# Five shorter steps for the substitution, three for the way back of the inverses, and a step of its own for the transposes

## The chip, the core and the metric

The kernel runs on one core of a Trainium2 chip. The time is the device time of the whole program, in microseconds (us), as a median of several runs. The profile shows one execution: the engines TensorE (PE, with its weight loads as PEld), VectorE (DVE), ScalarE (ACT), GpSimd (POOL) and SyncE (SP, which here issues every DMA). L794 is line 794 of the kernel.

## The reference

One layer of a decoder: the input x (2048 x 1024) is normalised and multiplied by one wide weight matrix. The result feeds three mixers: RWKV-7 time mixing with 8 heads of 64, a short convolution, and causal pooling; each is gated, multiplied by a branch matrix, merged by sigmoid gates, and goes through an output product. The change touches the RWKV part alone. There, in the reference,

```python
def _rwkv7_step(state, inp):
    r_t, w_t, k_t, v_t, a_t, b_t = inp
    sa = jnp.einsum('bhvk,bhk->bhv', state, a_t)
    state = (state * w_t[:, :, None, :] + sa[..., None] * b_t[:, :, None, :]
             + v_t[..., None] * k_t[:, :, None, :])
    y_t = jnp.einsum('bhvk,bhk->bhv', state, r_t)
    return state, y_t
```

runs over all 2048 positions.

## The kernel before, in words

**Main work.** The 2048 columns are worked in two halves. A list, `program` (L1221 to L1266), names the jobs in order: for each half the input projections of the RWKV part, of the convolution (8 pairs), of the pooling (4 pairs) and of the gates (12 pairs), and at the end the products that merge the branches and the output products. Almost every job is a `Pair` (L189): two column blocks of weights times two column blocks of data by Strassen's seven products. One `product` (L179) is 12 matmuls of 128x128 by 128x512: each number is split in a high and a low part, and three of the four products are taken. The weights come by DMA (L149), are split by ScalarE (L141) and GpSimd (L143), and `supply` (L162) keeps them up to five, three and two pieces ahead of their use. The results leave PSUM through ScalarE copies (L233, L238, L243) and VectorE additions (L247, L251, L255); two banks each (`ch` and `mm`) take them in turn.

**Slots.** After each product a job yields, and `execute` (L1280) then calls `supply`, issues the stores that are due (`after_product`), and advances the job's sides. A `Side` (L1076) is a generator with a rate: the rate is added to a credit at each slot, and the generator is called as often as the credit allows, at its first slot once more. At rate 1 that is one call per slot. Each engine executes in the order in which its instructions were issued, so a slot's side work stands ahead of the eviction of the product before it.

**Groups.** The RWKV part is a side: `rwkv_groups` (L674) works 16 groups of 128 positions, 8 in each half, in chunked form. The head (`group_head`, L595) loads and scales, the tail (`group_tail`, L639) normalises the output; the head of the next group and the tail of the one before run along in the group's steps. `step` (L688) yields to the main work, so the number of steps is the number of slots that a group takes: 25 in the first half and 24 in the second. In order of the steps `rwkv_group` (L683) does this:
- The matrices G by matmuls (L711) and a mask (L714), two steps. BK is turned by matmuls (L593), two steps; with them the 32x32 diagonal blocks are stored to DRAM (L734) and loaded back in another layout, NBt (L743). Two steps pass.
- The forward substitution for the inverses of 16x16 triangles (L751 to L757): 15 iterations on VectorE, each a product (L754) and a sum (L755), the operations shrinking from 120 to 8 elements a partition. A step follows j = 3, 7 and 11, and one the end, with which the next head starts.
- The inverses Tt go to DRAM (L763) and come back in the layout TT (L766), a step between. Then `step(3 if g < 8 else 2)` (L767).
- The inverses are put together to 64x64: transposes Td (L771), matmuls bx (L779), a ScalarE copy X (L782), matmuls by (L786), four ScalarE copies into TT (L790), two VectorE transposes T1 (L794), matmuls b1 (L805), copies M1 (L808), matmuls b2 (L812), copies into TT (L815). A step follows Td, X, T1, M1 and the last copies; by, its copies and T1 share one.
- Twice (two chunks of 64): matmuls and a copy R (L829, L832), matmuls and an operation U (L835, L837), matmuls for the new state bS and the output (L843 to L856), with a step after each.

The groups of the second half start with the last job of its RWKV projections and are ended by `groups[1].finish` ahead of the eighth merge job; those of the first half end by the last of the second half's RWKV projections. `finish` issues at once what is left. The loads of the second half's y (`late`, L1258) begin with the seventh merge job.

Of the kernel before, what the change touches and what calls it, by code (L numbers as in the profile page):

```python
# [23 lines left out]

OPS = ("B11", "T1", "T2", "B21", "B22", "T3", "T4")
NB = TH // BLK
# [27 lines left out]
def trunk_kernel(ctx, tc, x, pre_norm_w, post_norm_w, w_in, mu_shift, rwkv_w0, rwkv_w_up,  # L54
# [39 lines left out]
    def mm_bank():  # L94
        return ps.tile([P, BLK], F32, tag="mm", name="mm", bufs=2)
# [7 lines left out]
    def bc(ap, axis, n):  # L103
        u = ap.unsqueeze(axis)
        shape = list(u.shape)
        shape[axis] = n
        return u.to_broadcast(shape)
# [63 lines left out]
    def take():  # L171

        supply(1)
        taken[0] += 1
        return ready.pop(0)
# [3 lines left out]
    def product(bank, wt, op, start, stop=True):  # L179
        (hi, lo), (th, tl) = wt, op[:2]  # L180
        for k in range(HK):
            pe.matmul(bank, hi[:, k, :], th[k], start=start and k == 0, stop=False, skip_group_check=True)  # L182
            pe.matmul(bank, hi[:, k, :], tl[k], start=False, stop=False, skip_group_check=True)  # L183
            pe.matmul(bank, lo[:, k, :], th[k], start=False, stop=stop and k == HK - 1, skip_group_check=True)  # L184
# [4 lines left out]
    class Pair:  # L189
# [37 lines left out]
        def run(self):  # L227
# [6 lines left out]
            bb = mm_bank()  # L234
            product(bb, take(), ops["T1"], True)
            yield
# [52 lines left out]
    def single(ops, c, sink):  # L289

        def body():
# [6 lines left out]
            act.copy(p1[:, 16:], ba)  # L298
            product(bb, a1, h["T1"], True, False)
            yield  # L300
# [91 lines left out]
    def first_ops(x0):  # L392
# [18 lines left out]
        for j in range(4):  # L411
# [10 lines left out]
            def put(o, t, eng):  # L422
                hi, lo = ops[o]
                t3 = t.rearrange("p (k t) -> p k t", k=HK)
                act.copy(hi[:, :, c0], t3)
                ins = eng.tensor_tensor(lo[:, :, c0], t3, hi[:, :, c0].bitcast(F32), ALU.subtract).ins
                if eng is pool:
                    last_lo[0] = ins
# [7 lines left out]
            put("T2", t2, LO[2])  # L436
            put("T1", t1, LO[3])
            put("T3", t3, LO[4])
# [31 lines left out]
    def stage_sums(block, dst):  # L470

        for k in range(2 * HK):
# [8 lines left out]
            yield  # L481
            for o, out_, a, b in (("T1", B[0, 0], B[0, 1], B[0, 0]), ("T3", B[0, 1], B[1, 1], B[0, 1]),
                                  ("T2", B[1, 1], B[1, 1], B[0, 0]), ("T4", B[1, 0], B[1, 0], B[1, 1])):
# [190 lines left out]
    def rwkv_groups(gs):  # L674

        head = yield from group_head(gs[0])
        yield
        tail = iter(())
        for g in gs:
            head, tail = yield from rwkv_group(g, head, tail, g + 1 if g + 1 in gs else None)  # L680
        yield from tail

    def rwkv_group(g, head, before, following):  # L683
# [4 lines left out]
        def step(n=1, begin=False):  # L688
            if begin and following is not None:
                after[0] = group_head(following)  # L690
            for _ in range(n):
                next(before, None)
                if after[0] is not None:
                    try:
                        next(after[0])
                    except StopIteration as e:
                        after[0], got[0] = None, e.value
                yield
# [53 lines left out]
        for j in range(15):  # L752
            n = 15 - j
            dve.tensor_tensor(tmp[:, :, :n], bc(NBt[:, j, j + 1:], 1, 8), bc(Tt[:, :, j], 2, n), ALU.mult)  # L754
            dve.tensor_tensor(Tt[:, :, j + 1:], Tt[:, :, j + 1:], tmp[:, :, :n], ALU.add)  # L755
            if j in (3, 7, 11):
                yield from step()  # L757
        yield from step(1, True)
        tdf = td.rearrange("q a s t -> (q a) s t")
# [4 lines left out]
        yield from step()  # L764
        for q, (qs, bs_) in enumerate(quads):
            sp.dma_start(TT[qs, :, bs_], td[q].rearrange("a s t -> s a t"))  # L766
        yield from step(3 if g < 8 else 2)  # L767


        Td = rp.tile([P, 2 * NCT, 64], F32, tag="BK", name="Td")  # L770
# [16 lines left out]
        for q, (qs, bs_) in enumerate(quads):  # L787
            o = TT[q * 32:q * 32 + 16, :, q % 2 * 32 + 16:q % 2 * 32 + 32]
            i_ = byv[q * 32:q * 32 + 16, :, 16:32]
            act.copy(o, i_)  # L790
        T1 = rp.tile([P, 2 * NCT, 32], F32, tag="sc", name="T1")
        for h in range(2):
            s0 = slice(h * 64, h * 64 + 32)
            dve.transpose(T1[s0].rearrange("p a t -> p (a t)"), TT[s0, :, 0:32])  # L794
        yield from step()
# [144 lines left out]
    def mix_pooled(half):  # L940

        for i in range(NCT):
            pw = work("pw")[:, :P]
            sp.dma_start(pw, pool_w[i])
            for b in range(NB):
                t0 = half * TH + b * BLK
                pl, z = work("pl")[:, :BLK], work("z")[:, :BLK]
                sp.dma_start(pl, pD[:, i, t0:t0 + BLK])
                sp.dma_start(z, yD[2][:, i, t0:t0 + BLK])
                yield  # L950
                if b == 0:
                    pwh = wp.tile([P, P], F32R, tag="pwh", name="pwh", bufs=1)
                    act.copy(pwh, pw)
                    pwl = wp.tile([P, P], F32R, tag="pwl", name="pwl", bufs=1)
                    pool.tensor_tensor(pwl, pw, pwh.bitcast(F32), ALU.subtract)
                ph = wk.tile([P, BLK + 16], F32R, tag="wk", name="ph")[:, :BLK]
                act.copy(ph, pl)
                pr = pl.bitcast(F32R)
                dve.tensor_tensor(pr, pl, ph.bitcast(F32), ALU.subtract)
                yield  # L960
                bk = rk_bank()
                pe.matmul(bk, pwh, ph, start=True, stop=False)
                pe.matmul(bk, pwh, pr, start=False, stop=False)
                pe.matmul(bk, pwl, ph, start=False, stop=True)
                dve.scalar_tensor_tensor(z, bk, qps[:, i:i + 1], z, ALU.mult, ALU.mult)
                store(yD[2][:, i, t0:t0 + BLK], z)
                yield


    def gate_pair(half, h, n, d):  # L970
        def sink(e, b, val, tile_):
            t = work("gate")[:, :BLK] if tile_ is None else val
            act.activation(t, val, AF.Tanh, scale=0.5)
            t0 = half * TH + b * BLK
            store(gD[n][d + e, :, t0:t0 + BLK], t)

        return in_pair(h, OFF_GATE + n * D + d * P, OFF_GATE + n * D + (d + 1) * P, sink)
# [202 lines left out]
    def op_of(half):  # L1180
        return lambda: H[half]
# [41 lines left out]
    def job(j, *sides):  # L1223
        program.append((j, sides))

    groups = [Side(rwkv_groups(range(half * 8, half * 8 + 8)), 1) for half in range(2)]
    mixes = [Side(mix_pooled(0), 24 / 46), Side(mix_pooled(1), 24 / 80)]
    stages = [Side(stage_ops(1), 80 / 86), Side(stage_sums(wo_block, wD), 24 / 60)]
    first = proj(0)
# [2 lines left out]
    for half in range(2):  # L1232
# [8 lines left out]
        for n in (1, 2, 0):  # L1241
            for d in range(0, KT, 2):
                j = gate_pair(half, op_of(half), n, d)
# [26 lines left out]
    for entry in program:  # L1270
        if isinstance(entry, tuple):
            j = entry[0]
# [56 lines left out]
```

## Time and profile before

| | |
|---|---|
| median of 3 runs | 2333.09 us (2329.98 to 2333.73) |
| the profiled execution | 2330.51 us, its span 2328.8 us |
| mean granted TensorE clock | 0.961 of 2.4 GHz |
| instructions | 46956 |
| HBM | 206.08 MB read, 103.94 MB written |

The page has, for each engine, its busy time and share of the span, and then the span in 40 slices with the busy share of each in tenths; PEclk is the granted clock of TensorE in tenths. The view of waits names who waited for whom, with the total, the number and the longest. A view of windows gives, for stretches of the span, the busy time of each engine, the granted clock, and the load of the DMA engines. In the view of groups each row has busy time and mean ns of one, and then the idle time of the engine just ahead of them with what ended it.

### The profile page before, as it was taken

Reading aid. Unit: us, or ns where it says so; the run is one execution under the profiler, and the core shown is the slowest. Engines: PE = TensorE matmul, PEld = TensorE weight load, DVE = VectorE, ACT = ScalarE, POOL = GpSimd, SP = SyncE. Lnnn points to the kernel's source line nnn. Section 1 sums busy time; section 2 is a strip of 40 time slices with the busy share of each in tenths; the row PEclk is TensorE's granted clock in tenths of the full one; section 3 lists DMA queues with packets and bytes.
Section 4 is the critical chain, followed back from the end, with each engine's and each line's share of the span. In section 5 each row is a group of like instructions: output and inputs, shape, how many; then the busy total and the mean of one; then the engine's idle time right before and its main releaser. Section 6 shows DMA issues by size and latency. Waiting matters only on the chain.

```text
span 2328.8 us, 46956 instructions
## 1 busy us (share of the span) xinstructions
PE 2185.9 (94%) x18514; PEld 1759.5 (76%) x18514; DVE 1374.5 (59%) x2150; ACT 895.0 (38%) x1777; POOL 1365.0 (59%) x1137
## 2 busy tenths in 40 slices
PE   4999999989999999899989999999999999999897
PEld 4788777777787887768877787777877788787775
DVE  7413767676847637534576767846465653526554
ACT  5444433443434436344534433244343511314332
POOL 7657565665656555427656655446565355556775
PEclk7989999999999999979999999999999999999998
DMA  3244313253547427344432323346454765768443
GB/s 103 90 136 129 98 54 95 61 144 107 152 140 209 129 80 236 92 146 138 136 80 62 91 53 113 108 138 186 131 166 118 231 174 170 258 182 275 126 136 104
DMA packets 441207, 313.11 MB, mean 134 GB/s; under 512 B 105557, under 2 KB 362778, under 8 KB 440986
## 3 DMA queue, kind: packets, MB, share of 16 engines
q1 hardware_dynamic: 440986, 310.12, 44.5%
q8 instruction: 145, 2.38, 0.4%
q14 instruction: 76, 0.62, 0.1%
HBM read 206.08 MB, written 103.94 MB: 133 GB/s over the span
## 4 chain that ended last, share of the span: by engine, by line
PE 63%; DVE 14%; issue 5%; POOL 4%; DMA 4%; ACT 3%; SPq 1%; DVEq 0%; POOLq 0%; ACTq 0%
PE ch L182 10%; PE ch L183 9%; PE ch L184 9%; PE mm L182 8%; PE mm L183 7%; PE mm L184 7%; DVE Tt L755 3%; DVE Ttmp L754 3%; PE rk L593 2%; PE rk L711 2%; POOL wl L143 2%; POOL ws L212 1%; PE rk L835 1%; PE rk L827 1%; PE rk L843 1%
## 5 line engine op out<-in xcount | busy, mean ns | idle before, releaser
L143 POOL TENSOR_TENSOR wl<-ws,wh 128x512 fp32r<-128x512 f32 x484 | 674.0, 1395 | 548.1 <-ACT wh L141 514.0
L141 ACT CAST wh<-ws 128x512 fp32r<-128x512 f32 x484 | 298.7, 618 | 253.8 <-PE mm L183 91.3
L182 PE MATMUL ch<-hT,wh 128*128 128x512 f32 x864 | 358.0, 414 | 38.1 <-DVE p L255 30.9
L184 PE MATMUL ch<-hT,wl 128*128 128x512 f32 x864 | 344.8, 399 | 0.3 <-POOL wl L143 0.2
L183 PE MATMUL ch<-lT,wh 128*128 128x512 f32 x864 | 344.9, 399 | 0.1
L182 PE MATMUL mm<-hB,wh 128*128 128x512 f32 x600 | 241.6, 403 | 2.8 <-ACT p L298 2.8
L184 PE MATMUL mm<-hB,wl 128*128 128x512 f32 x600 | 234.3, 390 | 0.7 <-POOL wl L143 0.7
L183 PE MATMUL mm<-lB,wh 128*128 128x512 f32 x600 | 234.3, 391 | 0.0
L182 PEld LDWEIGHTS ch<-hT,wh 128*128 128x128 f32 x864 | 167.5, 194 | 83.3 <-issue 32.6
L143 POOL TENSOR_TENSOR wl<-s,wh 128x512 fp32r<-128x512 f32 x72 | 97.5, 1354 | 217.7 <-ACT wh L141 214.0
L212 POOL TENSOR_TENSOR ws<-ws,s 128x512 f32<-128x512 f32 x144 | 201.7, 1401 | 2.6 <-DMA ws<-in_w_in 2.6
L184 PEld LDWEIGHTS ch<-hT,wl 128*128 128x128 f32 x864 | 166.6, 193 | 38.1 <-POOL wl L143 1.3
L183 PEld LDWEIGHTS ch<-lT,wh 128*128 128x128 f32 x864 | 167.6, 194 | 32.5 <-issue 0.4
L1019 POOL TENSOR_TENSOR g<-g 128x512 f32<-128x512 f32 x64 | 86.4, 1353 | 108.0 <-DVE g L1015 95.9
L182 PEld LDWEIGHTS mm<-hB,wh 128*128 128x128 f32 x600 | 112.6, 188 | 29.7 <-ACT p L298 3.6
L182 PE MATMUL mm<-hT,wh 128*128 128x512 f32 x296 | 124.5, 421 | 10.6 <-DVE p L247 7.0
L184 PEld LDWEIGHTS mm<-hB,wl 128*128 128x128 f32 x600 | 112.7, 188 | 25.8 <-POOL wl L143 1.5
L183 PEld LDWEIGHTS mm<-lB,wh 128*128 128x128 f32 x600 | 112.7, 188 | 21.5
L184 PE MATMUL ch<-hB,wl 128*128 128x512 f32 x288 | 117.7, 409 | 10.5 <-POOL wl L143 10.5
L182 PE MATMUL ch<-hB,wh 128*128 128x512 f32 x288 | 120.8, 419 | 6.8 <-DVE g L1015 4.0
L755 DVE TENSOR_TENSOR Tt<-Tt,Ttmp 128x120 f32<-128x120 f32 (+14 forms) x240 | 117.4, 489 | 8.3
L184 PE MATMUL mm<-hT,wl 128*128 128x512 f32 x296 | 119.9, 405 | 1.0 <-POOL wl L143 0.8
(269 smaller groups left out, 4638.7 us busy)
## 6 DMA issues: line engine op xcount, KB each, us to landing
ws<-in_w_in SPq DMA_DIRECT2D x260, 256.0 KB
g<-gD SPq DMA_DIRECT2D x96, 256.0 KB
gD<-p SPq DMA_DIRECT2D x48, 256.0 KB
ly<-yD SPq DMA_DIRECT2D x48, 256.0 KB
ws<-in_w_branch SPq DMA_DIRECT2D x48, 256.0 KB
mD<-g SPq DMA_DIRECT2D x32, 256.0 KB
ws<-mD SPq DMA_DIRECT2D x32, 256.0 KB
xr<-in_x SPq DMA_DIRECT2D x32, 256.0 KB
```

Source lines behind the costliest of these rows:

```text
L141: act.copy(hi, src)
L143: pool.tensor_tensor(lo, src, hi.bitcast(F32), ALU.subtract)
L182: pe.matmul(bank, hi[:, k, :], th[k], start=start and k == 0, stop=False, skip_group_check=True)
L183: pe.matmul(bank, hi[:, k, :], tl[k], start=False, stop=False, skip_group_check=True)
L184: pe.matmul(bank, lo[:, k, :], th[k], start=False, stop=stop and k == HK - 1, skip_group_check=True)
L212: sums[0].tensor_tensor(w[o], w[a], w[b], op)
L593: both(lambda h, hs: pe.matmul(bank[hs, a * 64:a * 64 + 64], src[hs, a], ident[hs, hs], start=True, stop=True))
L711: both(lambda h, hs: pe.matmul(bgs[n][hs, i * P:(i + 1) * P], BK[hs, n, 2 * i + c], XA[hs, 2 * i + c].rearrange("p x t -> p (x t)"), start ...
L754: dve.tensor_tensor(tmp[:, :, :n], bc(NBt[:, j, j + 1:], 1, 8), bc(Tt[:, :, j], 2, n), ALU.mult)
L755: dve.tensor_tensor(Tt[:, :, j + 1:], Tt[:, :, j + 1:], tmp[:, :, :n], ALU.add)
L827: both(lambda h, hs: pe.matmul(r3[hs, i], G[hs, 1, 0, a], vt[hs, a], start=True, stop=False, skip_group_check=True))
L1019: pool.tensor_tensor(acc[b], acc[b], gs[b], ALU.add)
```

## The change

The substitution's steps follow j = 2, 5, 8 and 11 instead of 3, 7 and 11: five pieces of three iterations. After the reload of TT both halves pass three steps. A step is put between the copies into TT (L790) and the transposes T1. A group has 27 steps in both halves, and the side of the second half gets the rate 1.1. No instruction is added or taken away.

```diff
@@ -753,7 +753,7 @@
             n = 15 - j
             dve.tensor_tensor(tmp[:, :, :n], bc(NBt[:, j, j + 1:], 1, 8), bc(Tt[:, :, j], 2, n), ALU.mult)
             dve.tensor_tensor(Tt[:, :, j + 1:], Tt[:, :, j + 1:], tmp[:, :, :n], ALU.add)
-            if j in (3, 7, 11):
+            if j in (2, 5, 8, 11):
                 yield from step()
         yield from step(1, True)
         tdf = td.rearrange("q a s t -> (q a) s t")
@@ -764,7 +764,7 @@
         yield from step()
         for q, (qs, bs_) in enumerate(quads):
             sp.dma_start(TT[qs, :, bs_], td[q].rearrange("a s t -> s a t"))
-        yield from step(3 if g < 8 else 2)
+        yield from step(3)
 
 
         Td = rp.tile([P, 2 * NCT, 64], F32, tag="BK", name="Td")
@@ -788,6 +788,7 @@
             o = TT[q * 32:q * 32 + 16, :, q % 2 * 32 + 16:q % 2 * 32 + 32]
             i_ = byv[q * 32:q * 32 + 16, :, 16:32]
             act.copy(o, i_)
+        yield from step()
         T1 = rp.tile([P, 2 * NCT, 32], F32, tag="sc", name="T1")
         for h in range(2):
             s0 = slice(h * 64, h * 64 + 32)
@@ -1223,7 +1224,7 @@
-    groups = [Side(rwkv_groups(range(half * 8, half * 8 + 8)), 1) for half in range(2)]
+    groups = [Side(rwkv_groups(range(half * 8, half * 8 + 8)), (1, 1.1)[half]) for half in range(2)]
```

## Rows read from the trace of the kernel before

**Rows 1.** The page: busy time of each engine, and TensorE's clock in 40 slices.
```profile
PE 2185.9 (94%) x18514; PEld 1759.5 (76%) x18514; DVE 1374.5 (59%) x2150; ACT 895.0 (38%) x1777; POOL 1365.0 (59%) x1137
...
PEclk7989999999999999979999999999999999999998
```

**Rows 2.** Waits of TensorE, 250 to 1150 us: total us, times, longest.
```profile
PE rk L805 <- DVE T L794: 7.3, 3, 5.8
...
PE rk L779 <- DVE Td L771: 0.3, 1, 0.3
```

**Rows 3.** Waits of TensorE, 1150 to 1960 us.
```profile
PE rk L779 <- DVE Td L771: 10.5, 4, 3.8
...
PE rk L805 <- DVE T L794: 2.2, 2, 1.9
```

**Rows 4.** Five windows, TensorE: stretch, length, matmul time, granted clock, DMA share, GB/s.
```profile
296.00:306.00 10.00, 6.48 (x17) 0.66 0.08 10
...
1496.00:1507.00 11.00, 5.57 (x15) 0.69 0.68 205
sum 47.00, PE 28.14; mean PE 5.63
```

**Rows 5.** Further windows, TensorE, the columns as in rows 4.
```profile
611.00:618.00 7.00, 4.21 (x15) 1.00 0.45 124
905.00:914.00 9.00, 6.36 (x78) 0.62 0.93 261
521.00:535.00 14.00, 8.12 (x82) 0.63 0.29 95
921.00:927.00 6.00, 4.45 (x42) 0.72 1.04 329
1716.00:1721.00 5.00, 2.84 (x41) 1.00 0.16 60
1316.00:1327.00 11.00, 8.95 (x175) 0.69 0.05 14
1515.00:1525.00 10.00, 6.19 (x109) 0.83 0.62 184
1612.00:1624.00 12.00, 9.65 (x178) 0.72 0.90 270
1803.00:1812.00 9.00, 6.73 (x115) 0.81 0.75 215
1001.00:1030.00 29.00, 25.48 (x183) 0.53 0.59 190
```

**Rows 6.** Windows of the 16 chains: the chain's VectorE time, then all engines.
```profile
990.00:1007.00 17.00, 7.03 (x30) 0.85 0.13 36
...
sum 319.00, DVE 225.16; mean DVE 14.07
...
990.00:1007.00 17.00, 13.67 (x74) 9.62 (x73) 11.87 (x42) 6.98 (x13) 1.01 (x2) 0.85 0.13 36
...
sum 319.00, PE 290.71 PEld 234.37 DVE 294.32 ACT 98.73 POOL 166.12; mean PE 18.17 PEld 14.65 DVE 18.39 ACT 6.17 POOL 10.38
```

**Rows 7.** Timeline of VectorE and GpSimd at 1403 us: start, us, engine and line.
```profile
1403.10 0.18 DVE L754 TENSOR_TENSOR Ttmp<-NB,Tt 128x24 f32<-128x24 f32 x1
1403.31 1.28 DVE L755 TENSOR_TENSOR Tt<-Tt,Ttmp 128x24 f32<-128x24 f32 x1
...
1403.26 1.28 POOL L671 TENSOR_TENSOR d<-d,z 128x512 f32<-128x512 f32 x1 [4.96 <-DVE d L669]
```

**Rows 8.** Timeline of TensorE: the first matmuls of G in groups 9 and 10.
```profile
1267.18 1.92 PE L711 MATMUL rk<-XA,BK 64*64 64x128 f32 x32
...
1363.87 1.92 PE L711 MATMUL rk<-XA,BK 64*64 64x128 f32 x32
```

**Rows 9.** Groups on ScalarE and VectorE: busy us, mean ns, idle before, releaser.
```profile
L832 ACT COPY R<-rk 128x256 f32<-128x256 f32 x32 | 11.9, 372 | 99.0 <-PE rk L829 99.0
...
L794 DVE STREAM_TRANSPOSE T<-TT 32x256 f32<-32x256 f32 x32 | 13.9, 433 | 43.3 <-ACT TT L790 41.4
```

## The prediction

> **What bounds the kernel now.** I read the page first. TensorE's matmuls are busy 94% of the span, no other engine over 59% [rows 1]: the end is set by how densely one in-order stream of matmuls runs, so the change is worth what it saves in waits of TensorE, plus what TensorE loses after them in clock. 2328.8 - 2185.9 = 142.9 us of the span have no matmul. The line of the granted clock dips in many slices outside the start. The change touches no instruction, only the slot in which each is issued, so I went to the view of TensorE's waits, taken apart at 1150 us, where the groups of the second half begin. The first part [rows 2] has 7.3 us on the transposes T1 (L794) and 0.3 us on Td (L771); the second [rows 3] has 10.5 us on Td and 2.2 us on T1. The waits of the main products for evictions on VectorE stand in both. So Td, the first use of what the inverses' way back brings, is late only in the half that has two steps after the reload. Last I cut windows around each wait that belongs to a group's work [rows 4, 5]: length less matmul time is the wait, and twice (1 - granted clock) times length is the time at 1.2 instead of 2.4 GHz.
>
> **What those waits cost.** They fall into four kinds.
> (a) The substitution's chain. Its 30 small VectorE operations stand in front of the evictions in VectorE's order. Five windows [rows 4]: 47.0 - 28.1 = 18.9 us of waiting; three of them (from 296, 1404 and 1496 us) have 6.8 us each at the lower clock.
> (b) Weight pieces. The tail's product on GpSimd and the stores of Tt wait behind the same chain, and the weights wait behind those. Two windows (611, 905): 2.79 + 2.64 = 5.4 us, and 6.8 us of low clock.
> (c) T1. Copies, transposes and the matmuls that need them lie one product apart. Three windows (521, 921, 1716): 5.88 + 1.55 + 2.16 = 9.6 us, and 10.4 + 3.4 us of low clock.
> (d) Td. Four windows (1316, 1515, 1612, 1803): 2.05 + 3.81 + 2.35 + 2.27 = 10.5 us, and 6.8 + 3.4 + 6.7 + 3.4 = 20.3 us of low clock.
> At the low clock working time counts double, so a stretch costs half of what of it was work. How much of the wait lies inside it the rows don't say: for (d) the cost is between (20.3 - 10.5) / 2 = 4.9 and 20.3 / 2 = 10.2 us; I take 9, near the upper end, since these waits are short against the low stretches that go with them. In the same way (a) 8, (b) 3, (c) 5. With the waits: (a) 26.9, (b) 8.4, (c) 14.6, (d) 19.5, together 69.4 us. More than that the change can't give back.
>
> **Five steps of three.** A group's chain takes 225.2 / 16 = 14.1 us of VectorE; where GpSimd did almost nothing (the window from 990 us, 1.0 us of GpSimd) it took 7.0 us [rows 6]. The difference is single operations that take 1.28 instead of 0.18 us, as long as the GpSimd operation beside them [rows 7]. In the windows of the chains VectorE is busy 294.3 of 319 us [rows 6], so its queue is seldom empty there. Per slot the chain is 14.1 / 4 = 3.5 us now. If the waits behind GpSimd are shared out with the operations, it becomes 14.1 / 5 = 2.8 us; if each slot brings its own, it is (7.0 + 7.0 x 5/4) / 5 = 3.2 us. Between nothing and all of (a) and (b), 0 and 35.3 us, I take half, for the middle of 2.8 and 3.2: 17.7 us. What stays is late for the old reason, an eviction behind the chain.
> The Trainium skill, page "SBUF — State Buffer", section "Who interferes with whom", says that a VectorE operation with two SBUF inputs contends with a GpSimd operation that reads SBUF, and that whoever starts first keeps the shared ports for its whole instruction. By that rule the waits belong to the slot and the 3.2 us holds: a relief of 0.3 us a slot where I took 0.5, so 10.6 us instead of 17.7.
>
> **A step of its own for T1.** One more slot lies between the copies and b1. A slot of the second half is a group's 96.7 us (1267.18 to 1363.87 us, by the first matmuls of two groups [rows 8]) by its 24 steps, 4.0 us; (c) goes but for 5.88 - 4 = 2 us: 12.6 us back. Bounds: 0 if VectorE's queue is as deep one slot later, 14.6.
>
> **Three steps back in both halves.** Three slots instead of two lie between the reload and Td. In the second half this should do what it does in the first, where Td costs 0.3 us. But that half's side work now runs at 1.1: each tenth slot makes two calls. Counting the yields of the code, the first half has 236 slots and needs 11 + 8 x 27 + 10 = 237 calls (two in the first slot): it just fits, and its finish issues nothing. The second has 218 slots, 1 + 239 calls, and needs the same 237: it ends some three slots later than now (212 + 1 calls at rate 1), and the last rows of y are still stored before the late loads of them. So nothing piles up at either end, and I cost the ends at nothing; that cover is gone if a half had more calls than slots. After the first slot 21 slots are doubled. By the count, three of the eight groups of the half lose in such a slot the one that they gained for Td. I give (d) back by 5/8: 12.2 us; bounds 0 and 19.5.
>
> **What the doubled slots cost.** Of the 21, eight put two steps into one slot of which the second needs the first: R and U twice, U and bS, bS and R, bx and by, by and T1, T1 and b1, b1 and b2. TensorE then waits for a copy of 0.37 us on ScalarE or transposes of 2 x 0.43 us on VectorE [rows 9], if their queues are free; behind a queue, as T1 showed, for up to 5.8 us. I take 1.0 us, near the free end because ScalarE sat waiting for TensorE ahead of the copies of R, 99.0 us in all [rows 9]: 8 us. Three put six iterations of the chain into one slot: twice what (a) costs a group, 2 x 26.9 / 16 = 3.4 us, less the half that I have kept in the sum already, 2: 6 us. One (w and j0) makes VectorE wait for the substitution's input: 1.5 us. Four squeeze the stores and reloads and are in the 5/8, or, for the store of Tt in its chain's slot, keep SP's queue behind the chain; SP waits there in the same way today, and the weights are fetched five pieces ahead, so nothing. The other five are matmuls of G, transposes and head or tail: 1 us. Sum 16.5 us; bounds 5 (all queues free) and 40.
> One more place moves: the second single projection, 29 us at a clock of 0.53 [rows 5], with slots of six short matmuls. It now carries U, bS, R, U, bS and G, where it had the end of a chain, Td, bx and by. I take nothing, with 8 us either way.
>
> **Sum.** 17.7 + 12.6 + 12.2 - 16.5 = 26 us off. The profiled execution took 2330.5 us (span 2328.8), so 2304.5; it lies 2.6 us below the median of the three runs, 2333.1, and I expect 2306 us. With every bound for the change it is 2333 - 69 + 5 - 8 = 2261, with every one against it 2333 + 40 + 8 = 2381.
>
> **Rivals.**
> Less relief from the chain: each slot brings its own waits behind GpSimd and the chain still takes 3.2 us of it. The relief is 0.3 instead of 0.5 us a slot, 10.6 for 17.7 us: 19 us off, 2314. [...] For it stand the long operations of [rows 7]; against it, that a GpSimd operation met while no piece of the chain is in VectorE's queue delays nothing. Chance 0.13.
> More relief: a wait is all or nothing, and once VectorE's queue runs empty between pieces all of (a) to (d) goes, with the doubled slots at their free price: 69 - 5 = 64 us off, 2269. Against it: VectorE at 92% in these windows. Chance 0.12.
> Given back: with 27 steps every group meets other products than before, and as many collisions of chain and eviction come back in other places. (a) and (b) stay whole, (c) and (d) give 24.8 us, and with the doubled slots at 25 us, between my price and the upper bound, the sum is nil: 2333. For it: the waits of now are scattered over many places of the groups, which looks like chance. Chance 0.11.
> Slower, by the doubled slots of the second half. If a dependent pair costs what a Td wait costs, wait and clock, 19.5 / 4 = 4.9 us, nine of them eat the 42.5 us of gain; with twelve (eight dependent pairs, three chains, the input) it is 59 - 42.5 = 16 us slower, 2349. For it: waits of about 2 us did bring the clock down (the window from 1316 us). Against it: the copies of [rows 9] are short. Chance 0.14.
>
> **Numbers.** The forecast itself has 0.50. About 0.2%, 4.7 us, is what a measurement can tell from no change. Faster: 0.50 + 0.13 + 0.12 = 0.75; same 0.11; slower 0.14. The range must leave out 0.2: it drops most of the slower case and the far end of the good one, 2282 to 2336.
>
> **What would show it.** In the waits of the changed kernel T1 falls from 9.5 to under 4 us in all, Td to under 6 us, in the second half alone and in groups whose reload met a doubled slot; waits for p behind the chain halve. New, short waits appear for R, U, X, M and T1 every tenth slot. The matmul-free time falls from 143 to about 125 us and the mean clock rises from 0.961 to about 0.97. It is wrong if Td or T1 stay, if waits of over 2 us sit in doubled slots, or if as much waiting turns up at evictions elsewhere.

## The result, and the profile after

The changed kernel took 2354.14 us in the median of 4 runs (2352.01 to 2356.68), the kernel before 2331.53 us beside it: a ratio of 1.0102, with an interval from 1.0081 to 1.0124. It is 1% slower where 1.1% faster was forecast, and lies outside the range. The profiled execution took 2352.3 us, its span 2350.6 us.

The page of the changed kernel, busy time and clock, to be set beside [rows 1]:

```profile
PE 2179.4 (93%) x18514; PEld 1757.3 (75%) x18514; DVE 1401.9 (60%) x2150; ACT 895.2 (38%) x1777; POOL 1365.1 (58%) x1137
...
PEclk7989999999999999999999999999999999999999
```

TensorE works 6.5 us less, since the mean clock rose from 0.961 to 0.964, and yet has 2350.6 - 2179.4 = 171.2 us without a matmul, where it had 142.9. So the loss is waits, 28.3 us more of them. VectorE is busy 27.4 us longer with the same 2150 instructions. The view of groups has for the chain (busy us, mean ns of one, idle before), in the kernel before

```profile
L755 DVE TENSOR_TENSOR Tt<-Tt,Ttmp 128x120 f32<-128x120 f32 (+14 forms) x240 | 117.4, 489 | 8.3
L754 DVE TENSOR_TENSOR Ttmp<-NB,Tt 128x120 f32<-128x120 f32 (+14 forms) x240 | 108.2, 451 | 7.7 <-DMA NB<-nd 1.1
```

and in the changed one

```profile
L754 DVE TENSOR_TENSOR Ttmp<-NB,Tt 128x120 f32<-128x120 f32 (+14 forms) x240 | 129.6, 540 | 6.2 <-DMA NB<-nd 0.2
L755 DVE TENSOR_TENSOR Tt<-Tt,Ttmp 128x120 f32<-128x120 f32 (+14 forms) x240 | 124.0, 517 | 8.2
```

The two lines together went from 225.6 to 253.6 us, 28.0 us: as much as all of VectorE's extra time. A group's chain takes 253.6 / 16 = 15.85 us instead of 14.1.

The waits of TensorE, to be set beside [rows 2] and [rows 3] (total us, times, longest). Three lines of the kernel before that these rows leave out, first from 250 to 1150 us, then from 1150 to 1960 us:

```profile
PE ch L182 <- DVE p L255: 3.7, 2, 3.4
PE mm L182 <- DVE p L247: 3.5, 1, 3.5
PE ch L182 <- ACT u L243: 1.9, 1, 1.9
...
PE ch L182 <- DVE p L255: 9.2, 4, 5.4
PE mm L182 <- DVE p L247: 3.5, 1, 3.5
PE ch L182 <- ACT u L243: 1.1, 1, 1.1
```

In the changed kernel from 250 to 1150 us (lines behind L790 are one higher than before):

```profile
PE ch L182 <- DVE p L255: 24.6, 6, 13.0
PE mm L182 <- DVE p L247: 6.2, 2, 4.0
PE rk L964 <- DVE pl L960: 5.4, 1, 5.4
PE rk L846 <- DVE U L838: 3.2, 3, 1.6
PE rk L806 <- DVE T L795: 3.1, 1, 3.1
...
PE rk L779 <- DVE Td L771: 2.5, 2, 2.1
```

and from 1150 to 1960 us:

```profile
PE ch L182 <- DVE p L255: 17.0, 5, 6.2
PE ch L182 <- ACT u L243: 9.3, 3, 6.3
PE rk L806 <- DVE T L795: 3.7, 6, 2.1
...
PE mm L182 <- DVE p L247: 2.4, 1, 2.4
...
PE rk L779 <- DVE Td L771: 1.7, 1, 1.7
```

The waits that the change was aimed at are smaller: Td from 10.8 to 4.2 us in the two parts, T1 from 9.5 to 6.8. But p behind VectorE (L255) was 3.7 and 9.2 us in these parts of the kernel before, and is 24.6 and 17.0; u behind ScalarE was 1.9 and 1.1, and is 9.3 in the second part alone. Between the first and the last group of each half, all waits of TensorE over 0.15 us added up went from 44.3 to 55.1 and from 30.4 to 44.8 us: 25 of the 28 us.

**The longest wait.** TensorE waits 12.97 us, to 943.37 us, for one p: it belongs to the second half's first pair of RWKV projections, whose last product stands behind the first two of the second pair. Without it the first part's waits add up to 42.1 us, less than the 44.3 of the kernel before. VectorE's timeline ahead of it (start, duration in us):

```profile
926.52 1.33 DVE L754 TENSOR_TENSOR Ttmp<-NB,Tt 128x72 f32<-128x72 f32 x1
...
930.04 0.69 DVE L669 TENSOR_TENSOR d<-d,v 128x512 f32<-128x512 f32 x1
930.64 2.50 DVE L358 TENSOR_TENSOR lT<-lT,hT 128x512 fp32r<-128x512 f32 x4
...
937.79 1.18 DVE L754 TENSOR_TENSOR Ttmp<-NB,Tt 128x40 f32<-128x40 f32 x1
939.00 1.18 DVE L755 TENSOR_TENSOR Tt<-Tt,Ttmp 128x40 f32<-128x40 f32 x1
940.22 1.18 DVE L754 TENSOR_TENSOR Ttmp<-NB,Tt 128x32 f32<-128x32 f32 x1
941.44 1.19 DVE L755 TENSOR_TENSOR Tt<-Tt,Ttmp 128x32 f32<-128x32 f32 x1
942.55 0.67 DVE L255 TENSOR_TENSOR p<-p,ch 128x512 f32<-128x512 f32 x1
```

In these slots VectorE also splits the operands of the next half (L358, 2.5 us) and scales the shifted projections. A piece of the chain of group 6 stands right ahead of the p that TensorE needs, and each of its operations takes 1.18 us or more, about as long as the GpSimd operations beside it (1.25 us each). In the kernel before that chain ended at 898.3 us, just ahead of such splits:

```profile
898.12 0.17 DVE L755 TENSOR_TENSOR Tt<-Tt,Ttmp 128x8 f32<-128x8 f32 x1
```

Here it begins 41 us later (919.8 instead of 878.7 us), among them.

**A second kind.** At 1533.69 us TensorE waits 6.25 us for a ScalarE copy of u, and ScalarE 8.12 us for a buffer whose last content, silu, is still to be stored. SyncE's queue at that time:

```profile
1525.19 1.81 SPq L763 DMA_DIRECT2D td<-Tt  x4
1528.94 1.78 SPq L766 DMA_DIRECT2D TT<-td  x4
1530.76 0.45 SPq L329 DMA_DIRECT2D yD<-silu  x1
```

The store of Tt could go only when the chain had ended at 1525.16 us; the load back waits for that store, and the store of silu stands behind both, in the queue's order.

### The profile page after: what moved, and what is told of

It reads as the page before. It is cut to its first block, busy times and chain, and to the rows that moved or that the text cites. A ratio compares the mean times of both kernels' runs of the same rounds, so it can differ in the third digit from the quotient of the medians.

```text
span 2350.6 us, 46954 instructions
## 1 busy us (share of the span) xinstructions
PE 2179.4 (93%) x18514; PEld 1757.3 (75%) x18514; DVE 1401.9 (60%) x2150; ACT 895.2 (38%) x1777; POOL 1365.1 (58%) x1137
## 4 chain that ended last, share of the span: by engine, by line
PE 35%; DVE 11%; issue 4%; POOL 3%; DMA 3%; ACT 2%; SPq 1%; POOLq 0%; DVEq 0%; ACTq 0%
PE ch L182 5%; PE ch L183 5%; PE ch L184 5%; PE mm L182 4%; PE mm L183 4%; PE mm L184 4%; DVE Ttmp L754 2%; DVE Tt L755 2%; POOL wl L143 1%; PE rk L593 1%; PE rk L711 1%; POOL ws L212 1%; DMA ws<-mD 1%; DVE p L1060 1%; DVE hB L484 1%
## 5 line engine op out<-in xcount | busy, mean ns | idle before, releaser
L754 DVE TENSOR_TENSOR Ttmp<-NB,Tt 128x120 f32<-128x120 f32 (+14 forms) x240 | 129.6, 540 | 6.2 <-DMA NB<-nd 0.2
L755 DVE TENSOR_TENSOR Tt<-Tt,Ttmp 128x120 f32<-128x120 f32 (+14 forms) x240 | 124.0, 517 | 8.2
```

## The experiments

All ran beside the kernel before. Five pieces are cuts at j = 2, 5, 8 and 11, four at 3, 7 and 11, three at 4 and 9. Each ratio is to runs of the kernel before on the same chip (medians of 2324.8 to 2332.9 us), with its 95% interval. The edits are combined out of these lines: the five pieces; the third step before Td; T1's own step, ahead of its transposes; and Tt in PSUM, with a copy of it that the stores read.

```diff
-            if j in (3, 7, 11):
+            if j in (2, 5, 8, 11):    
-        yield from step(3 if g < 8 else 2)
+        yield from step(3)
+        yield from step()
-        Tt = rp.tile([P, 8, 16], F32, tag="sa", name="Tt")
+        Tt = rk_bank()[:, :128].rearrange("p (a t) -> p a t", a=8)
+        Ts = rp.tile([P, 8, 16], F32, tag="sa", name="Ts")
+        act.copy(Ts, Tt)
```

| kernel | steps a group, 1st/2nd half | rate of the 2nd | Tt in SBUF: us, ratio [interval] | Tt in PSUM: us, ratio [interval] |
|---|---|---|---|---|
| before | 25/24 | 1 | 2331.5, 1 | 2292.2, 0.9805 [0.9769, 0.9842] |
| three pieces | 24/23 | 1 | 2346.2, 1.0050 [1.0036, 1.0065] | 2299.0, 0.9851 [0.9825, 0.9876] |
| five | 26/25 | 1 | 2344.8, 1.0079 [1.0053, 1.0104] | 2316.8, 0.9938 [0.9918, 0.9957] |
| T1 | 26/25 | 1 | 2340.3, 1.0036 [1.0018, 1.0053] | 2290.3, 0.9816 [0.9781, 0.9852] |
| third step | 25/25 | 1 | not run | 2295.7, 0.9858 [0.9826, 0.9890] |
| five, third step | 26/26 | 1.06 | 2340.8, 1.0037 [1.0023, 1.0051] | 2295.3, 0.9840 [0.9818, 0.9862] |
| T1, third step | 26/26 | 1.06 | 2342.4, 1.0064 [1.0038, 1.0089] | 2297.2, 0.9862 [0.9831, 0.9893] |
| all three (the change) | 27/27 | 1.1 | 2354.1, 1.0102 [1.0081, 1.0124] | 2304.4, 0.9903 [0.9876, 0.9931] |
| the change in the second half alone | 25/27 | 1.1 | 2345.9, 1.0054 [1.0031, 1.0077] | |
| empty steps | 27/27 | 1.1 | 2371.7, 1.0185 [1.0154, 1.0216] | |

By the count of the yields a second half of 25 steps at rate 1 needs two calls more than it has; its end issues the last two of the tail at once. The labels: with Tt in SBUF five is e1, T1 and the third step e2, the empty steps e3, the second half alone e6, T1 e8, three pieces e10, five and the third step e18. The four-slot shift below is e5. With Tt in PSUM the whole change is e4, the kernel before e7, three pieces e12, five e13, T1 e14, the third step e15, T1 and the third step e16, five and the third step e17.

The expectations name three explanations. Theory L: the chain of the substitution became longer, since each slot that it is spread over brings its own waits behind GpSimd. Theory P: the steps of the groups now stand beside other main work, and this place decides what they delay. Theory D: the doubled slots of the rate 1.1 cost the time.

### Parts of the change, and its length

Five pieces alone, the change without them, and the kernel before with empty steps at the end of each group instead of the change, which are these:

```diff
             yield from step()
+        yield from step(2 if g < 8 else 3)
         for _ in before:
```

> The kernel before with the substitution in five pieces of three and nothing else; rate 1 in both halves, 26 and 25 steps. Theory L (the chain's own length: each slot that it is spread over brings its own waits behind GpSimd, so five slots make it longer and keep the evictions behind it for longer): chains of 15.5 to 16 us of VectorE a group instead of 14.1, and slower than before by 8 to 20 us, 2340 to 2352. Theory P (places: a group of 27 steps puts its chains on other main work, such as the fills of the next half's operands, and that sets the waits): somewhere else than before and after, within 10 us of before, and the chain's time by what it meets. Theory D (doubled slots of the rate 1.1 cost it): no doubled slot but the first, so 2320 to 2333.

> The changed kernel with the substitution in four pieces as before (26 steps in both halves, rate 1.06 in the second, 12 or 13 doubled slots). Theory L: the chain is 14 us again and T1 and Td give what they promised: 2310 to 2325. Theory P: anywhere from 2320 to 2350, with the waits at places where a chain meets fills or pooling. Theory D: about half of the change's loss, 2340 to 2348.

> The kernel before with as many steps as the changed one, but all the added ones empty and between two groups: 27 steps in both halves, rate 1.1 in the second, the same 21 doubled slots. Theory L: the chain stays at 14 us and the time within 8 us of before, 2325 to 2340, the doubled slots costing a few us. Theory P: the groups stand on the same products as in the changed kernel at their starts, so its loss comes back: 2345 to 2360. Theory D: the same, 2345 to 2360, but with the waits in doubled slots; P has them elsewhere.

Five pieces alone were 0.79% slower; they don't relieve. The chain took 242.4 us. Without them the change still lost 0.64%. The empty steps, which cut the chain no finer and give neither T1 nor Td more time, lost most, 1.85%, more than any theory had forecast, and TensorE's longest wait is the one shown above, for the same pair:

```profile
PE ch L182 <- DVE p L255: 56.4, 16, 13.3
PE rk L779 <- DVE Td L771: 21.9, 9, 4.0
```

It is 13.35 us long, beside a group of the first half, where no slot behind the first is doubled. So two more steps a group are enough for the longest wait, whatever they hold: they carry every later step of a half past other products.

The change in the second half alone, and T1's step alone:

> The change in the second half alone; the first half's groups have 25 steps as before. From the stages of the trace the changed kernel lost 7 us in the first half's groups and 16 us from the second half's on. Theory P and D: 14 to 18 us slower than before, 5 to 9 us faster than the changed kernel. Theory L shares the loss evenly, 11 us in each half: 10 to 12 us slower than before.

> The kernel before with a step of its own for T1 alone (26 and 25 steps, rate 1). The prediction's term (c) gives 12 us: 2313 to 2320 against a before of about 2328. Theory P: the waits at T1 go down by about 7 us, but every group after the first stands one slot later for each group, and the chains' waits change by up to 20 us either way: 2315 to 2350, more likely slower. Theory L: 2313 to 2325.

The second half alone carries 0.54 of the 1.02%, so about half of the loss arises in the first half, at rate 1. T1's step alone took its wait away (9.5 to 1.7 us) and brought others: Td rose from 10.8 to 20.7 us, with 6.24 us in one place of the first half and 8.21 us in one of the second.

Is it the place in time itself? The second half's groups of the kernel before, begun four slots later:

```diff
+        for _ in range(4 if gs[0] else 0):
+            yield
         head = yield from group_head(gs[0])
```

> The kernel before, with the groups of the second half begun four slots later; steps, rate and chains as before. Theory P (what a chain costs is set by the main work that it meets: the last pooling and first gate jobs, and the fills of the next operands): the second half's groups stand on other products, so its waits change by as much as in the changed kernel, 5 to 20 us slower than before. Theory L (the chain's length by its number of slots): within 4 us of before. Theory D (doubled slots): within 4 us of before, there is none but the first.

It took 2332.28 us, 0.9992 [0.9979, 1.0005]. The kinds of the half's waits changed (the main products' waits for VectorE from 16.3 to 10.3 us, for ScalarE from 1.1 to 4.4), their sum did not, 30.4 us in both. Theory P had forecast 5 to 20 us for it. This shift cost nothing; what is left is more steps, or other distances between them.

Fewer pieces:

> The kernel before with the substitution in three pieces (cuts after j = 4 and 9; 24 and 23 steps). Theory L: chains of 12 to 13.3 us of VectorE a group, as fewer slots bring fewer waits behind GpSimd; each piece is longer, so evictions wait longer at a time: within 8 us of before. Theory P: chains about as long, and other places: 5 to 20 us slower, with waits at evictions. If every added step costs by itself, whatever it holds, one step less gains: 5 to 12 us faster than before.

The chain fell to 200.5 us, 12.5 a group, and the kernel was still 0.50% slower, with 17.4 us of Td in the second half. With three and four pieces a group's chain takes 12.5 and 14.1 us, with five 15.2 (e1; 14.6 in e18, 15.9 in the change): each slot brings some of the waits behind GpSimd. The place counts as well: four pieces took 13.6 us a group in e5 and 15.0 in e3, the latter as long as five. And the time does not follow the chain.

### The splits of L358 on GpSimd

```diff
-            dve.tensor_tensor(lo, raw, hi.bitcast(F32), ALU.subtract)
+            pool.tensor_tensor(lo, raw, hi.bitcast(F32), ALU.subtract)
```

in the changed kernel (e9), and in the one before with Tt in PSUM (e11).

> The changed kernel with the low parts of the loaded operands (the fills, 13 products of operands by 4 subtractions) computed on GpSimd instead of VectorE. Theory P: the wait of 13.0 us in the first half, where group 6's chain meets the fills, goes down to under 4 us, with the 3.6 us at the end of the second half's gates, 10 to 18 us faster than the changed kernel in all unless GpSimd then delays the weights. Theory L: the chain is longer still, since GpSimd works more beside it, and the wait stays: no faster than the changed kernel.

> The kernel before with Tt in PSUM and the fills on GpSimd. If the crowded places are VectorE's alone: 5 to 12 us faster than with Tt in PSUM alone, 2280 to 2288. If GpSimd is as crowded there (weights late): no gain or a loss of up to 10 us.

They took 2383.10 us, 1.0205 [1.0177, 1.0233], and 2322.27 us, 0.9950 [0.9933, 0.9967], 1.0 and 1.5 points slower than without this edit, and the second slower than either of its expectations. The long wait fell from 13.0 to 7.1 us, but GpSimd went from 1365 to 1482 us of work, the chain to 267.3 us, and the weights, which GpSimd splits too, came late. In the waits of e9 they are, where the changed kernel has 7.5 us on the second line:

```profile
PE mm L184 <- POOL wl L143: 15.3, 6, 6.0
PE ch L184 <- POOL wl L143: 12.4, 5, 6.9
```

The splits are in front of that p in the timeline, and without them the wait is shorter; how much of the 13 us is theirs this run does not tell, since the rest of the schedule moved too. That they decide the loss is not shown.

### The chain without its waits

> The changed kernel with Tt kept in PSUM while the substitution runs, and copied to SBUF by ScalarE before its DMA: every operation of the chain has one SBUF input instead of two. If the long chain operations are waits for a port that GpSimd holds and if the chain's length is what costs (theory L): chains of 6 to 9 us of VectorE a group instead of 15.9, VectorE's busy time down by 100 to 150 us, and a time of 2280 to 2320. Theory P or D: chains shorter too, but the time stays above 2335. If the long operations are not such waits: chains of 15 us or more, and no change against the changed kernel.

> The kernel before with Tt in PSUM during the substitution, as in the run of the changed kernel that held it there. Theory L: with 7 us chains the number of pieces matters no more; the same gain as the changed kernel had from it, 48 us, would be too much, since its chains were longer: 25 to 40 us faster than before, 2288 to 2305. Theory P: shorter chains meet less of the crowded places, and the places of the kernel before are the better ones: 2280 to 2300, faster than the changed kernel with the same edit. If the PSUM form costs something of its own: above 2310.

With Tt in PSUM an operation of the chain has one SBUF input. VectorE beside a GpSimd operation in e7:

```profile
1194.87 0.17 DVE L754 TENSOR_TENSOR Ttmp<-NB,rk 128x24 f32<-128x24 f32 x1
1195.07 0.19 DVE L755 TENSOR_TENSOR rk<-rk,Ttmp 128x24 f32<-128x24 f32 x1
1195.30 0.17 DVE L754 TENSOR_TENSOR Ttmp<-NB,rk 128x16 f32<-128x16 f32 x1
1195.51 0.18 DVE L755 TENSOR_TENSOR rk<-rk,Ttmp 128x16 f32<-128x16 f32 x1
...
1194.36 1.74 POOL L143 TENSOR_TENSOR wl<-ws,wh 128x512 fp32r<-128x512 f32 x1
```

Against [rows 7] nothing waits: the chain takes 108.6 us in all, 6.8 a group, close to the 7.0 us that [rows 6] showed where GpSimd did almost nothing. The edit is worth 1.95% in the kernel before and 1.99 points in the changed one, some 45 us in either; it also keeps one of the banks of `rk` busy through the chain and adds a copy, which no run tests apart. The difference between the two stays: 0.9903 against 0.9805. So the chain's waits are not why the change loses: the theory that its longer chain is the cause fell with these two. In e4, the schedule of the change with the short chain, TensorE still waits for the p of the longest wait, but 5.82 instead of 12.97 us (the view names what stood next to that p in VectorE's order):

```profile
917.34 0.77 PE L182 MATMUL ch<-hT,wh 128*128 128x512 f32 x1 [5.82 <-DVE Ttmp L754]
```

So some 7 of the 13 us went with the chain's waits behind GpSimd, and 5.8 stayed with the other work that stands there.

### Five pieces with a short chain

With the chain's waits out of the way, the parts again:

> The kernel before with Tt in PSUM and the substitution in three pieces. With chains of 6.8 us the pieces are short enough: within 5 us of four pieces, 2287 to 2297; if each step costs by itself, 5 to 10 us faster, 2280 to 2287.

> The kernel before with Tt in PSUM and the substitution in five pieces; rate 1 in both halves. With Tt in SBUF five pieces lost 0.8%. Theory L (that loss is the chain's waits behind GpSimd, about 1.8 us for every slot that it is spread over): nothing is lost against four pieces in PSUM, 2286 to 2297. Theory P (it is one more slot a group, which puts the groups' steps on other main work): the same loss as with Tt in SBUF, 2303 to 2315.

> The kernel before with Tt in PSUM and a step of its own for T1; rate 1. With Tt in SBUF that lost 0.36% while the chains kept their 14.1 us. Theory P: the same 5 to 12 us are lost here, 2297 to 2306, with Td late where it meets the pooling and the fills. Theory L: with short chains ahead of it Td is not late, so T1 gives its 7 to 10 us: 2282 to 2288.

> The kernel before with Tt in PSUM and three steps of the way back in the second half, at rate 1 and so without doubled slots. Term (d) of the prediction, Td, is 4.8 us in the waits of this kernel without the step: 3 to 8 us gained if nothing else moves, 2284 to 2290. Theory P: Td gives its wait and other waits come where the groups of the second half now stand: 2290 to 2305.

> The changed kernel with Tt in PSUM and four pieces (26 steps, rate 1.06). Theory L: as the changed kernel with Tt in PSUM, 2300 to 2308, since the pieces no longer matter. Theory P: between that and the kernel before with Tt in PSUM, 2293 to 2303. Theory D (doubled slots): half of the 12 us between those two goes, 2297 to 2300.

Five pieces lost 1.3 points though the chain is as short as with four (108.6 us). T1's step alone costs nothing here (0.9816). Three pieces, the third step, and T1 with the third step measured about half a point more than the kernel before with Tt in PSUM, with intervals that overlap its own. T1's step fell between the ranges of the two theories, the third step into that of theory P, T1 with the third step into those of P and D; five pieces lost a little more than P had forecast. The waits of TensorE in e13 from 1150 to 1960 us:

```profile
PE ch L182 <- DVE p L255: 17.7, 3, 13.1
PE rk L781 <- DVE Td L773: 15.4, 6, 4.8
```

The 13.1 us look like an eviction behind work, but VectorE had none. Its own timeline there (in brackets the idle time and what ended it):

```profile
1794.02 0.67 DVE L251 TENSOR_TENSOR u<-u,mm 128x512 f32<-128x512 f32 x1
1805.91 0.71 DVE L773 STREAM_TRANSPOSE Td<-TT 128x512 f32<-128x512 f32 x1 [11.22 <-DMA TT<-td]
1806.54 0.65 DVE L255 TENSOR_TENSOR p<-p,ch 128x512 f32<-128x512 f32 x1
```

and SyncE's queue:

```profile
1793.31 3.03 SPq L765 DMA_DIRECT2D td<-Ts  x4
1796.44 2.17 SPq L351 DMA_DIRECT2D ly<-yD  x4
1798.65 0.43 SPq L149 DMA_DIRECT2D ws<-in_w_branch  x1
1799.13 0.50 SPq L329 DMA_DIRECT2D gD<-gate  x1
1799.73 2.07 SPq L768 DMA_DIRECT2D TT<-td  x4
```

ScalarE had copied the chain's result long before:

```profile
1785.08 0.26 ACT L760 COPY Ts<-rk 128x128 f32<-128x128 f32 x1
```

VectorE stands 11.22 us before Td, the main p behind it in its order. The store td went out 8.0 us after that copy, behind the next group's loads and loads of y in SyncE's queue; the reload TT went out 6.4 us behind the store, with loads of y and others between, and had then to land. With the 15.4 us these are 26.6 us of waits for the reload; in e7 the half lost 4.8 us on Td. Five pieces alone had the same in SBUF (e1: 12.0 us of Td, and 9.82 us of VectorE's idle time ahead of Td at 1832.85 us). If that is the whole loss, the third step must take it away:

> Tt in PSUM, five pieces of the chain, and the third step before Td in both halves (T1 as before, the second half at rate 1.06). In the short-chain kernel with five pieces (2316.8 us) the matmuls of the second half waited 15.4 us for Td at bx, and 11.2 us for an eviction that stood behind Td in VectorE's order while Td's loads stood behind fills of y in SP's queue; without the five pieces (2292.2 us) it was 4.8 us in all. Theory that the loss of the five pieces in the short-chain kernel is this one reload: with the third step these waits fall under 8 us, and the time is 2292 to 2302 us. Rival, that a schedule with more steps loses the same in other places: the reload's waits fall and others of 10 us and more take their place, 2308 to 2322 us.

> The change without T1's own step, everything in SBUF: five pieces and the third step before Td in both halves, the second half at rate 1.06. With the five pieces alone it was 2344.8 us, and 12.0 + 9.8 us of the second half's waits were Td's reload. Theory that the reload alone carries that loss: 2325 to 2332 us, no slower than before. Theory that the place of the groups' steps against the full slots decides: the reload's waits go and others come, 2338 to 2355 us, as all other schedules with 26 or 27 steps a group did.

With the short chain it does: 2295.33 us, 0.9840 [0.9818, 0.9862], from 0.9938, in the range of the first theory, and its interval overlaps that of e7. The waits of e17 in the second part:

```profile
PE ch L182 <- DVE p L255: 6.4, 2, 4.0
PE rk L612 <- ACT sq L603: 3.5, 1, 3.5
PE ch L182 <- ACT u L243: 3.5, 1, 3.5
PE rk L781 <- DVE Td L773: 2.8, 1, 2.8
```

In SBUF (e18) it took 2340.80 us, inside the range of the second theory: the third step gave 0.42 points of the 0.79 back and 0.37% stayed. By these medians the reload was about half of that loss. The second part of e18 has 4.0 us of waits for Td, but 7.6 us for u, where the kernel before had 1.1, and 7.3 us for the head's sq, where it had none.

## Why the prediction was wrong

**What bounds the kernel** held: the time followed TensorE's waits, 28.3 us more of them and 6.5 us less work.

**Five steps of three** is the step that failed. I let half of (a) and (b), 17.7 us, go, with a lower bound of nothing. Alone (e1) the five pieces made the kernel 0.79% slower, some 18 us. In the change the evictions by VectorE (L255 and L247) rose from 7.2 to 30.8 us in the first part and from 12.7 to 19.4 in the second. Two things were wrong. The chain of a slot came near the less favourable value: 253.6 / 16 / 5 = 3.17 us (3.0 in e1, 2.9 in e18), where the rival had 3.2. By the Trainium skill, page "SBUF — State Buffer", section "Who interferes with whom", VectorE's operation of two SBUF inputs contends with a GpSimd operation that reads SBUF, and one with a single SBUF input does not; the 0.17 us operations of e7 beside GpSimd agree. That such waits go with the slots was my inference from it: 12.5, 14.1 and 15.2 us for three, four and five pieces agree, the 15.0 us of e3's four pieces do not. And this rival gave 2314 us, since it too took a shorter slot for a relief. That was the larger error: I worked a mean load a slot into a gain, where the waits are a few collisions of a step with a crowded product. The five pieces move all later steps of the half by one slot a group; there Td's reload met the loads of y in SyncE's queue (13.2 us in e1), and in the changed kernel the chain of group 6 met the splits and the projections (13.0 us). A loss was to be had there, and my bound had none. SyncE's queue I costed only for the store of Tt, at nothing.

**A step of its own for T1**: the wait fell from 9.5 to 6.8 us, not to 2; 3.7 us of it in the second half, where it had been 2.2. The step alone cost 0.36% (e8), where 12.6 us were to be gained; there Td's waits took up what T1's gave.

**Three steps back**: the size came out near, by luck. 6.6 of 10.8 us went, where I gave 5/8. But I had three groups of the second half lose the gain in a doubled slot, and the first half unchanged. The second half gave 8.8 of its 10.5 us, and the 1.7 us that stayed are in group 13 (to 1736.52 us), whose reload met no doubled slot; the first half rose from 0.3 to 2.5 us. With a short chain and five pieces the step brings 0.98 points (e13 to e17), about 23 us, more than the 12.2 predicted; alone (e15) it brings nothing: the half's waits at bx for Td went from 4.8 to 0.3 us, but 8.9 us of p came, in 4.9 of which VectorE stood before Td. Its worth depends on where the other steps put the reload.

**The doubled slots**: the dependent pairs were priced about right. TensorE's waits in them are 2.89 us (bx and by, at 1334.57 us), 2.12 (T1 and b1), 0.89 (b1 and b2) and three of about 0.5 (R and U twice, U and bS), 7.4 us for my 8; the first two are waits of over 2 us in doubled slots, which I had named as a sign of being wrong. Of the three doubled pieces of chain, one has a long wait close behind it (group 11: j = 0 to 5 in one go from 1503.27 us, then 6.24 us for p, to 1514.01 us), but the same group had one of 5.43 us in the kernel before. By its own words (3.4 us each, less half of 1.7) the term for these three comes to 7.6 us, not 6. No run has the whole change with and without doubled slots, so their cost in time is not measured. The rival that ended slower had the sign, and not the mechanism: the first half has none behind its first slot and carries its part of the loss (e6 leaves it out and loses half). The ends cost nothing, as predicted. The second single projection took 29.4 us from the first to the last of its groups of six matmuls, 24.6 before, though most matmuls took 0.39 instead of 0.63 us: 4.8 us lost, inside the 8 either way.

**Given back**, with 0.11, was nearest: collisions came back in other places. It had as many collisions return as there were; more did. Of the 27-step schedules (e3, the change, e4) all lose about a point or more against the kernel with the same Tt and 25/24 steps. Why 27 steps meet the full products worse than 25 is shown for single waits (943, 1533 and, with five pieces, 1807 us) and not as a rule: no run moved one of those products away. The parts do not add up, which is what places would do: with Tt in SBUF the third step takes 0.42 points off after the five pieces (e1 to e18) and adds 0.28 after T1's step (e8 to e2); with Tt in PSUM it takes 0.98 off (e13 to e17) and adds 0.46 (e14 to e16). Fewer steps lost too (e10), and of the nine other schedules with Tt in SBUF none was faster than the kernel before. Its schedule may be one that had been picked for its good places; the record does not say how it came about, so this stays open.

## What to carry to other kernels

Where side work is dealt out by slots, a cut finer or a step more is a new schedule for all that follows: look up what each moved step meets in the queues of its new place, and let the range of the estimate reach into a loss, instead of counting on a mean relief. If TensorE waits for an eviction, look whether the evicting engine worked or stood itself: behind p there was a chain once and a DMA the other time, and the remedies differ. Making the chain short was worth more than any placing of it: one operand in PSUM, with one copy more, took 1.95% off the kernel before (2292.18 us; with T1's step 2290.29, the two not to be told apart), and these are the fastest versions here.

## What the runs showed of the hardware

A small operation of VectorE (128x24) with two SBUF inputs took 1.28 us beside a GpSimd operation of 1.28 us and 0.18 us without one [rows 7]; with one input in PSUM it took 0.17 to 0.19 us beside GpSimd (e7). I knew the first; that half of a group's 14.1 us would go with one operand (to 6.8), for 3.2 us more of ScalarE's busy time (898.4 us in e4, 895.2 in the changed kernel), I had not expected.
